# A two-layer diffusion backbone on one core: the first adaLN group in blocks of 128 channels, the S5 setup behind the modulation, and two adaLN groups moved from layer 0 to layer 1

## The chip, the cores and the metric

The kernel runs as one program on one core of a Trainium2 chip. The metric is device time in microseconds of one execution; the times below are of three executions. One execution was also taken with the hardware profiler, and all rows are from that one.

## The reference, cut to what matters

Two layers work on 256 context tokens and 256 latent tokens of 1024 channels, in float32. Every layer begins with the adaLN parameters, six rows of 1024 numbers for each of the two streams:

```
mod = silu(cond) @ w_ada + b_ada          # (1024) @ (1024 x 6144), for c and for c_ctx
h   = layer_norm(x) * (1 + mod[1]) + mod[0]
z   = h @ w_in                            # S5, latent attention, window attention, three gates
y   = merge(s5(z0), mla(z1..3), window(z4..6), gates(z7)) @ w_out
x   = layer_norm(ALPHA * x + mod[2] * y)
f   = expert_choice_ffn(layer_norm(x) * (1 + mod[4]) + mod[3])     # 16 experts, SwiGLU
x   = layer_norm(ALPHA * x + mod[5] * f)
```

Only `mod[0]` (shift) and `mod[1]` (scale) are needed for `h`; the other four are needed after the mixers. Layer 1 updates the latent stream alone. The S5 mixer also needs tables made of its own parameters (discretised states, products of B and C with powers), which depend on no token: the code calls their making the S5 setup.

## The kernel before, in words

`build` runs the layers one after the other. `w_ada` of one layer is 24 MB; it is used in three groups of 8 MB, group 0 for `mod[0:2]`, group 1 for `mod[2:4]`, group 2 for `mod[4:6]`. `ada_group` takes a group in eight steps of 1 MB. Step k holds input channels 128k to 128k+127 for all 2048 outputs of the group, so no output is complete before the eighth step; then the bias is added, four transposes follow, and `modT` is written. A step is 16 matmuls with 32 columns of `silu(cond)` as the weights.

Group 0 of layer 0 is made at the very start, into seven tiles of its own and two buffers of `stg`, a ring of four buffers of 512 KB that all weights of `w_in` pass through too. The four `x` tiles are loaded after the fifth step's weights. `layer` then loads the rest of the constants (`const[:, 128:]`, 985 KB), and `modulated_split` does the layer norm, and for each channel block k transposes, scales and shifts it and splits it into a high and a low part (`h`); after every second block the closure `step` of `s5_product` issues two blocks of the S5 input product, 24 matmuls (12 for each block).

`s5_setup` is a generator in two parts. The first part (small operations on 32 columns) is traced at the very start. The second part, which builds B and C products in the blocks `big0` to `big2`, is traced after the S5 product and its transposes (`s5_inputs`), and ahead of `proj_tok`, which projects the attention inputs. `s5_main`, the S5 scan in eight turns, needs everything of it.

The build step makes a list schedule for each engine: of the instructions that are ready in its own time model, the one traced earliest goes first. So work traced later moves forward into idle time unless something holds it, and loads whose buffers are free leave in the order of the code. `keep_in_program_order` pins an instruction behind the one traced before it on its engine. SyncE issues all loads. PSUM tiles come from named sets; "sc" has two, "tp" two, "ad" one.

The other adaLN groups are queued in `adaq`. The gate and branch matmuls are queued in `fillq`, and `tick` in the S5 and attention loops issues some of them. In `step` each piece of fill work adds its modelled time to `ada_debt`, and adaLN steps (1.6 each) are issued until the debt is paid. Five groups stand in the queue of layer 0 (its own 1 and 2, and all three of layer 1), none in layer 1. `drain(True)` issues what is left at the end of the mixers. 16 KB per partition at the top of the arena, called "late", are reserved for what comes after the mixers, and hold nothing until then.

After the mixers come the output projection, the router and the 16 experts (12 MB of weights each, loaded through buffers that become free one by one).

Of the kernel before, what the change touches and what calls it, by code (L numbers as in the profile page):

```python
# [15 lines left out]
KT = 8  # L16
DEPTH = 2
# [140 lines left out]
class Net:  # L158
# [48 lines left out]
    def step(self):  # L207
        try:
            us = next(self.fillq[0])
            self.debt -= us  # L210
            self.ada_debt += us
        except StopIteration:
            self.fillq.pop(0)
        while self.adaq and self.ada_debt > 0:
            try:
                self.ada_debt -= next(self.adaq[0])
            except StopIteration:
                self.adaq.pop(0)
# [129 lines left out]
        nc.vector.tensor_scalar(self.sc.rearrange("p (k s) -> p k s", s=32)[:, :, 0:2],  # L348
                                t2.rearrange("p (k s) -> p k s", s=2), 0.5, None, op0=OP.mult)

    def ada_group(self, l, g, bufs=None):

        nc = self.nc
        R = self.adarow[(l + g) % 2]
        self.load(R, self.ins["b_rep"][l, g])
        pt = self.ps("ad")
        scv = self.sc.rearrange("p (k s) -> p k s", s=32)
        src = self.ins["w_ada"][l, g]
        for k in range(KT):
            if bufs and k < 7:  # L360
                self.load(bufs[k], src[k])
                ws = [bufs[k][:, 0:1024], bufs[k][:, 1024:2048]]
            else:
                ws = []
                for h in range(2):
                    ws.append(self.stg())
                    self.load(ws[h], src[k, :, 1024 * h:1024 * h + 1024])
            for h in range(2):
                for j in range(4):

                    i = self.mm(pt[32 * j:32 * j + 32, 256 * h:256 * h + 256], scv[:, k, :],
                                ws[h][:, 256 * j:256 * j + 256], k == 0 and h == 0, k == KT - 1)
                    if k == 0 and h + j:
                        self.tc.keep_in_program_order(i)
            yield 1.6
        nc.vector.tensor_tensor(R, pt, R, op=OP.add)
        tp = self.ps("tp")
        for b in range(4):
            self.tr(tp[:, b * 128:(b + 1) * 128], R[:, b * 128:(b + 1) * 128])
        tv = tp.rearrange("p (b jj jm s) -> p jj jm b s", b=4, jj=2, jm=2)  # L380
        for jj in range(2):
            m = 2 * g + jj
            dst = self.modT[l % 2][:, m].rearrange("p (jm b) s -> p jm b s", jm=2)
            self.nc.vector.tensor_copy(dst, tv[:, jj, :, :, 0:2])
            if m in (1, 4):
                nc.vector.tensor_scalar(self.modT[l % 2][:, m], self.modT[l % 2][:, m], 1.0, None, op0=OP.add)
        self.adaR[l % 2, g] = True
        yield 0.0

    def mod_row(self, l, m, s, dst, scale=1.0):  # L390
# [77 lines left out]
    def modulated_split(self, l, x, in_place, step, stats):  # L468

        nc = self.nc  # L470
        mt = self.modT[l % 2]
        xns = {}
        for t in range(4):
            xns[t] = x[t] if in_place[t] else self.buf(f"xn{t}", D)
            if t in stats:
                self.ln_final(xns[t], x[t], *stats[t])
            else:
                self.ln_apply(xns[t], x[t])
        step(None, None)
        hh, hl = [self.block(f"h{r}", F32R).rearrange("p (k n) -> p k n", k=KT) for r in range(2)]  # L480
        part = lambda k, c: (hh[:, k, c], hl[:, k, c])
# [2 lines left out]
        units = [(k, s) for k in range(KT) for s in range(2)] if l == 0 else [(k, s) for s in range(2) for k in range(KT)]  # L484
        for u in range(0, 16, 2):
            (k, s), (k1, s1) = units[u:u + 2]
            if s1 and k1 > 2 and k1 % 2:
                step(part, (k1 - 3) // 2)
            tp, h = self.ps("tp"), tmps()
            for i, (k, s) in enumerate(units[u:u + 2]):  # L490
                for t in range(2):
                    self.tr(tp[:, 256 * i + 128 * t:256 * i + 128 * t + 128], xns[2 * s + t][:, k * 128:(k + 1) * 128])
            for i, (k, s) in enumerate(units[u:u + 2]):
                c = slice(256 * i, 256 * i + 256)
                scale, shift = mt[:, 1, k, s:s + 1], mt[:, 0, k, s:s + 1]
# [9 lines left out]
        step(part, 3)  # L505
        self.unrot(htmp=3)
        self.free(*[f"xn{t}" for t in range(4) if not in_place[t]])
        return part
# [2 lines left out]
    def s5_setup(self, l, S, NP):  # L511

        nc = self.nc
        v, g = nc.vector, nc.gpsimd
        bg = [self.block(f"big{i}", F32) for i in range(3)]
        CE = S["CE"] = [t[:, 0:2560].rearrange("p (d j e h) -> p d j e h", d=2, j=16, e=5) for t in bg[:2]]
        BM = S["BM"] = [[t.rearrange("p (j c) -> p j c", j=16) for t in ts]
                        for ts in ([t[:, 2560:3584] for t in bg[:2]], [bg[2][:, 1024 * d:1024 * d + 1024] for d in range(2)])]
        MM = S["MM"] = [t[:, 3584:4096].rearrange("p (x q c) -> p x q c", x=2, q=4) for t in bg[:2]]
# [22 lines left out]
        n = [0]  # L542
# [63 lines left out]
        v.scalar_tensor_tensor(fr, kk, MAGIC, fr, op0=OP.subtract, op1=OP.subtract)  # L606
        v.tensor_scalar(S["fr"], fr, -1.0, None, op0=OP.mult)
        yield
        load_part(0)
        QQ = part(64).rearrange("p (r d j) -> p r d j", r=2, d=2)  # L610
        qrv, qiv = QQ[:, 0], QQ[:, 1]
        v.tensor_copy(QQ[:, 0].rearrange("p d j -> p (d j)"), qr)
        v.tensor_copy(QQ[:, 1].rearrange("p d j -> p (d j)"), qi)
        KX = part(4 * 112).rearrange("p (q i h) -> p q i h", q=4, i=7)
        BB = part(64 * NP).rearrange("p (r d j h) -> p r d j h", r=2, d=2, j=NP)
        X1 = part(64 * NP).rearrange("p (k j h) -> p k j h", k=4, j=NP)
# [1073 lines left out]
    def build(self, layers=(0, 1), stop=None):  # L1690
# [3 lines left out]
        with tc.tile_pool(name="main", bufs=1) as main, \  # L1694
# [12 lines left out]
            self.adaR, self.OH, self.ah, self.cd, self.back, self.norm, self.rw, self.rrow = {}, {}, {}, {}, {}, {}, {}, {}  # L1707
            self.buf("late", 4096, at=self.LATE)
            self.adarow = [self.buf(f"ada{i}", 512, low=True) for i in range(2)]
            x = {t: self.buf(f"x{t}", D, low=True) for t in range(4)}  # L1710
            self.ada_start()
# [5 lines left out]
            hb = [self.block(f"h{i}", F32) for i in range(2)]  # L1717
            bufs = [hb[i // 2][:, 2048 * (i % 2):2048 * (i % 2) + 2048] for i in range(4)]
            bufs += [self.block(f"extra{i}", F32)[:, 0:2048] for i in range(2)] + [self.buf("wada", 2048, True)]
            for k, _ in enumerate(self.ada_group(layers[0], 0, bufs)):  # L1720
                if k == 4:
                    for t in range(4):
                        self.load(x[t], self.xin(t))
                if k in (7, 8):
                    kc = len(self.early)
                    self.early.append(self.wload(self.w_in(layers[0], 0, 512)[:, 2 * kc:2 * kc + 2], 2, 512))
            self.free("wada")
            for l in layers:
                self.layer(l, x, 1 if l == 0 and 1 in layers else None)
            for t in (2, 3):  # L1730
                self.load(self.out[0, (t - 2) * 128:(t - 1) * 128], x[t])

    def xin(self, t):
        return self.ins["ctx" if t < 2 else "x"][0, (t % 2) * 128:(t % 2) * 128 + 128]

    def layer(self, l, x, nxt):
        tc, nc = self.tc, self.nc
        full = l == 0
        q0 = 0 if full else 256
        N = 512 - q0  # L1740
        with tc.tile_pool(name=f"parts{l}", bufs=1, reuse_waits="tile") as self.R:
            if l:
                self.stg = self.rot("stg", 1024, 3, at=20288)
            step, pts = self.s5_product(l)
            if (l % 2, 1) not in self.adaR:
# [5 lines left out]
                pass  # L1751
            S = self.S
            Z = self.proj_tok(l, h, full)
            if (l % 2, 1) not in self.adaR:
                self.adaq += [self.ada_group(l, 1), self.ada_group(l, 2)]
            if nxt is not None:
                self.adaq += [self.ada_group(nxt, g) for g in range(3)]
            mT = self.buf("mT", KT * N, True, 12416 if full else None).rearrange("p (k n) -> p k n", k=KT)
            self.fill(self.gates(l, h, 0, mT, q0))
            if not full:  # L1760
# [78 lines left out]
        with tc.tile_pool(name=f"late{l}", bufs=1, reuse_waits="tile") as pool:  # L1839
# [22 lines left out]
            self.T = {}  # L1862
            tts = (0, 1, 2, 3) if full else (2, 3)
            self.free(*[n for n in self.A.live if n[0] in "EF"])
            self.buf("late", 4096, at=self.LATE)
            self.finish(l, x, pts, nxt is not None)

    ARENA_COLS = 27456
# [19 lines left out]
def _prepare(inputs):  # L1888
# [11 lines left out]
    a["w_ada"] = f("w_ada").reshape(DEPTH, KT, 128, 3, 4, 2, 256).transpose(0, 3, 1, 2, 5, 4, 6).reshape(DEPTH, 3, KT, 128, 2048)  # L1900
# [54 lines left out]
```

## Time and profile before

| | |
|---|---|
| median of three executions | 2099.42 us (2098.45 to 2099.58) |
| the profiled execution's own time | 2097.34 us |
| its span, first to last instruction | 2095.6 us |
| busy in the span: TensorE matmul | 1791.9 us (86%) |
| VectorE | 1042.9 us (50%) |
| ScalarE | 611.3 us (29%) |
| GpSimd | 451.5 us (22%) |
| read from HBM | 541 MB |

PE is TensorE's matmuls, PEld its weight loads, DVE is VectorE, ACT ScalarE, POOL GpSimd, and SPq the queue of SyncE, which issues the loads. An engine's busy share is a mean over stages that have different limits, so the stretches of the rows further down are to be read one by one. In them, the granted clock is TensorE's as a share of full speed, and the DMA share is the mean over the 16 DMA engines. Most matmuls are on the helper's line 243 and most loads on line 229, so a group is told apart by the tiles that it names.

### The profile page before, as it was taken

To read this page: it belongs to the slowest core of one execution; us is meant where nothing else is said; L and a number is where in the kernel's file an instruction comes from. 1 tells how busy PE (TensorE), PEld (TensorE's weight loads), DVE (VectorE), ACT (ScalarE), POOL (GpSimd) and SP (SyncE) were. 2 spreads that over 40 slices of the span, in tenths; PEclk is the share of its full clock that TensorE was granted. 3 is DMA by queue.
4 is the path that set the end of the run, shared out by engine and by line. 5 is a ranking of instruction groups with operands and counts; after the bars stand their busy time and mean duration, and the time that the engine had idled before them with its cause. 6 is when DMAs were issued, how large, how long until landed. Compare 5 with 4: busy or idle time off the path is not lost.

```text
span 2095.6 us, 31733 instructions
## 1 busy us (share of the span) xinstructions
PE 1791.9 (86%) x12425; PEld 1112.2 (53%) x12425; DVE 1042.9 (50%) x2431; ACT 611.3 (29%) x1353; POOL 451.5 (22%) x590
## 2 busy tenths in 40 slices
PE   5899899999999699999799979799998776676765
PEld 2876666677777544434233368787786532232221
DVE  6767666756528712313555367977767321010102
ACT  2444253344424311101111165654553110000000
POOL 5735320011125100001343034641114000000000
PEclk8999999999999799999999989999999888776777
DMA  9236744522247689999999733342267799999996
GB/s 334 67 123 218 245 144 163 163 78 71 60 132 274 248 354 421 421 421 416 416 413 351 297 91 94 81 129 63 76 214 297 291 420 421 421 421 421 420 421 272
DMA packets 173013, 544.20 MB, mean 260 GB/s; under 512 B 18624, under 2 KB 101696, under 8 KB 122816
## 3 DMA queue, kind: packets, MB, share of 16 engines
q1 hardware_dynamic: 172864, 542.18, 68.2%
q8 instruction: 98, 1.61, 0.3%
q14 instruction: 51, 0.42, 0.1%
HBM read 541.09 MB, written 1.05 MB: 259 GB/s over the span
## 4 chain that ended last, share of the span: by engine, by line
PE 54%; DMA 23%; DVE 14%; POOL 3%; ACT 3%; issue 3%; SPq 0%; POOLq 0%; ACTq 0%; DVEq 0%
PE sc L243 16%; PE mm L243 16%; PE F L243 13%; DMA arena<-in_w_down 4%; DMA arena<-in_w_up 4%; PE tp L246 4%; PE ad L243 4%; DMA arena<-in_w_gate 3%; DVE extra L852 2%; DVE wc L407 2%; DMA h<-in_w_gate 2%; DMA big<-in_w_gate 2%; DMA arena<-in_w_in 1%; DMA extra<-in_w_up 1%; DMA extra<-in_w_gate 1%
## 5 line engine op out<-in xcount | busy, mean ns | idle before, releaser
L243 PE MATMUL F<-h,wc 128*128 128x256 f32 (+1 forms) x1200 | 237.1, 350 | 11.3 <-ACT arena L1295 9.0
L404 ACT ACTIVATE wc<-arena 128x512 fp32r<-128x512 f32 (+2 forms) x280 | 169.9, 619 | 208.6 <-DMA arena<-in_w_in 45.8
L407 DVE TENSOR_TENSOR wc<-arena,wc 128x512 fp32r<-128x512 f32 (+2 forms) x205 | 163.3, 808 | 112.9 <-ACT wc L404 112.5
L243 PE MATMUL sc<-arena,xs 128*32 128x256 f32 (+1 forms) x1336 | 188.5, 522 | 33.7 <-DMA arena<-in_w_up 20.5
L243 PEld LDWEIGHTS F<-h,wc 128*128 128x128 f32 x1200 | 188.5, 196 | 42.6 <-ACT arena L1295 9.9
L243 PE MATMUL mm<-arena 128*32 128x256 f32 (+5 forms) x1244 | 186.1, 467 | 21.9 <-DMA arena<-in_w_down 13.4
L246 PE MATMUL tp<-const,arena 128*128 128x128 f32 (+2 forms) x819 | 137.5, 293 | 70.4 <-DVE arena L1618 11.6
L1641 DVE TENSOR_TENSOR arena<-mm,arena 32x512 f32<-32x512 f32 (+1 forms) x128 | 70.9, 554 | 219.0 <-PE mm L243 217.4
L407 POOL TENSOR_TENSOR wc<-arena,wc 128x512 fp32r<-128x512 f32 (+2 forms) x75 | 96.9, 1292 | 376.3 <-ACT wc L404 316.7
L246 PEld LDWEIGHTS tp<-const,arena 128*128 128x128 f32 (+2 forms) x819 | 97.3, 147 | 130.5 <-issue 38.5
L238 ACT ACTIVATE arena<-tp 128x512 f32<-128x512 f32 (+3 forms) x142 | 61.9, 463 | 341.7 <-PE tp L246 297.4
L260 POOL TENSOR_TENSOR lnq<-lnq,k 128x1 f32<-128x1 f32 x22 | 16.5, 750 | 568.8 <-DVE lnq L307 530.0
L243 PEld LDWEIGHTS sc<-arena,xs 128*32 128x32 f32 (+1 forms) x1336 | 60.8, 131 | 139.7 <-issue 68.7
L243 PEld LDWEIGHTS mm<-arena 128*32 128x32 f32 (+2 forms) x1244 | 76.3, 137 | 107.2 <-issue 50.5
L243 PE MATMUL sc<-h,xs 128*32 128x256 f32 (+1 forms) x752 | 112.3, 533 | 21.0 <-DMA h<-in_w_gate 13.2
L1618 DVE TENSOR_TENSOR arena<-arena,sc 128x512 f32<-128x512 f32 (+1 forms) x32 | 17.7, 554 | 178.2 <-PE sc L243 177.9
L243 PE MATMUL sc<-big,xs 128*32 128x256 f32 (+1 forms) x632 | 80.8, 487 | 25.2 <-DMA big<-in_w_gate 13.0
L1616 ACT ACTIVATE arena<-sc 128x512 f32<-128x512 f32 (+1 forms) x32 | 15.7, 491 | 295.1 <-PE sc L243 295.1
L243 PE MATMUL mm<-wc,h 128*128 128x512 f32 (+2 forms) x288 | 79.1, 399 | 11.3 <-ACT h L496 4.4
L243 PE MATMUL F<-extra,wc 128*128 128x256 f32 (+1 forms) x432 | 85.7, 343 | 3.5 <-DVE arena L1330 3.1
L1617 DVE SCALAR_TENSOR_TENSOR arena<-arena,sc 128x512 f32<-128x512 f32 (+1 forms) x32 | 17.7, 554 | 142.3 <-ACT arena L1616 142.2
L243 PEld LDWEIGHTS sc<-h,xs 128*32 128x32 f32 (+1 forms) x752 | 36.8, 133 | 89.2 <-issue 60.7
(344 smaller groups left out, 3183.1 us busy)
## 6 DMA issues: line engine op xcount, KB each, us to landing
arena<-in_w_up SPq DMA_DIRECT2D x65, 1024.0 KB, 16.8
arena<-in_w_down SPq DMA_DIRECT2D x61, 1024.0 KB, 19.8
arena<-in_w_gate SPq DMA_DIRECT2D x48, 1024.0 KB, 19.7
arena<-in_w_ada SPq DMA_DIRECT2D x82, 512.0 KB, 5.0
h<-in_w_gate SPq DMA_DIRECT2D x41, 1024.0 KB, 15.0
arena<-in_w_in SPq DMA_DIRECT2D x66, 512.0 KB, 4.0
big<-in_w_up SPq DMA_DIRECT2D x26, 1024.0 KB, 19.8
h<-in_w_down SPq DMA_DIRECT2D x26, 1024.0 KB, 18.6
```

Source lines behind the costliest of these rows:

```text
L238: self.nc.scalar.activation(out, in_, AF.Copy)
L243: return self.nc.tensor.matmul(out, lhsT, rhs, start=start, stop=stop, skip_group_check=True)
L246: self.nc.tensor.transpose(out, in_, self.c("idn")[:n, :n])
L260: self.nc.gpsimd.tensor_tensor(out, in_, e.to_broadcast(list(in_.shape)), op=OP.pow)
L404: nc.scalar.activation(hi, src, AF.Copy)
L407: eng.tensor_tensor(lo, src, hi.bitcast(F32), op=OP.subtract)
L852: v.tensor_tensor_scan(z, rb, z, 0.0, op0=OP.mult, op1=OP.add)
L1616: nc.scalar.activation(th, gu[0][:, :NF], AF.Tanh, scale=0.5)
L1617: v.scalar_tensor_tensor(th, th, 1.0, gu[0][:, :NF], op0=OP.add, op1=OP.mult)
L1618: v.tensor_tensor(th, th, gu[1][:, :NF], op=OP.mult)
L1641: v.tensor_tensor(YS[n][o:o + 32, c * NF:(c + 1) * NF], yp[r:r + 32, :NF], m5[r:r + 32], op=OP.mult)
```

## The change

1. **First group in blocks.** The weights of group 0 of layer 0 are laid out anew: tile b holds all 1024 input channels for outputs 128b to 128b+127 of shift and scale. `ada_first` is a generator; each call makes one block: eight matmuls, a copy to SBUF, two small matmuls that add the four row groups and turn the result, and one addition of the bias from a small new array `b_t` into `modT`. `modulated_split` calls it ahead of each channel block. The `x` tiles are loaded first, then the eight tiles of weights into `big0` to `big2`, `extra0`, `extra1` and "late", with the first two chunks of `w_in` among them. Two of the four layer norms of layer 0 are applied by ScalarE in place of VectorE.
2. **S5 setup behind the modulation.** The blocks `big0` to `big2` are taken for the setup only at the start of its second part, and in layer 0 the two copies at its head are pinned behind what VectorE was given before them.
3. **Groups of layer 1.** Layer 0 queues three groups (its own 1 and 2, and group 0 of layer 1), layer 1 queues its groups 1 and 2. Their loads go through buffers of their own in "late" (four in layer 0, three in layer 1) in place of `stg`. The debt grows by 0.35 of the fill time in layer 0 and by 0.2 in layer 1.

```diff
             us = next(self.fillq[0])
             self.debt -= us
-            self.ada_debt += us
+            self.ada_debt += us * self.ADA
...
-    def ada_group(self, l, g, bufs=None):
+    def ada_first(self, l, tiles):
+
+        nc = self.nc
+        v = nc.vector
+        own = self.buf("adafirst", 532)
+        bt, two = own[:, 512:528].rearrange("p (m k) -> p m k", m=2), own[:, 528:530]
+        self.load(bt, self.ins["b_t"])
+        v.tensor_scalar(bt[:, 1], bt[:, 1], 1.0, None, op0=OP.add)
+        v.tensor_reduce(two, self.c("idn").rearrange("p (j s) -> p s j", j=4)[:, 0:2], axis=AX.X, op=OP.add)
+        scv = self.sc.rearrange("p (k s) -> p k s", s=32)
+        for b in range(KT):
+            pt = self.ps("sc")
+            for r in range(2):
+                for j in range(4):
+                    k = 4 * r + j
+                    self.mm(pt[32 * j:32 * j + 32, 0:256], scv[:, k, :], tiles[b][:, 256 * k:256 * k + 256], r == 0, r == 1)
+            R = own[:, 256 * (b % 2):256 * (b % 2) + 256]
+            self.copy(R, pt[:, 0:256], "v")
+            for m in range(2):
+                self.mm(pt[:, 256 + 2 * m:258 + 2 * m], R[:, 128 * m:128 * m + 128], two, True, True)
+            v.tensor_tensor(self.modT[l % 2][:, 0:2, b], pt[:, 256:260].rearrange("p (m s) -> p m s", m=2),
+                            bt[:, :, b, None].to_broadcast([128, 2, 2]), op=OP.add)
+            yield
+        self.free("adafirst")
+
+    def ada_group(self, l, g):
...
-            if bufs and k < 7:
-                self.load(bufs[k], src[k])
-                ws = [bufs[k][:, 0:1024], bufs[k][:, 1024:2048]]
-            else:
-                ws = []
-                for h in range(2):
-                    ws.append(self.stg())
-                    self.load(ws[h], src[k, :, 1024 * h:1024 * h + 1024])
+            ws = []
+            for h in range(2):
+                ws.append(self.astg())
+                self.load(ws[h], src[k, :, 1024 * h:1024 * h + 1024])
...
-                self.ln_apply(xns[t], x[t])
+                self.ln_apply(xns[t], x[t], "va"[t % 2])
...
             (k, s), (k1, s1) = units[u:u + 2]
+            next(self.first, None)
...
-        v.tensor_copy(QQ[:, 0].rearrange("p d j -> p (d j)"), qr)
-        v.tensor_copy(QQ[:, 1].rearrange("p d j -> p (d j)"), qi)
+        for i, q in enumerate((qr, qi)):
+            c = v.tensor_copy(QQ[:, i].rearrange("p d j -> p (d j)"), q)
+            if NP == 16:
+                self.tc.keep_in_program_order(c)
...
-            self.buf("late", 4096, at=self.LATE)
+            late = self.take_late(4)
...
-            for k, _ in enumerate(self.ada_group(layers[0], 0, bufs)):
-                if k == 4:
-                    for t in range(4):
-                        self.load(x[t], self.xin(t))
-                if k in (7, 8):
+            for t in range(4):
+                self.load(x[t], self.xin(t))
+            tiles = []
+            for i in range(3):
+                big = self.block(f"big{i}", F32)
+                tiles += [big[:, c:c + 2048] for c in range(0, int(big.shape[1]), 2048)]
+            tiles += [self.block(f"extra{i}", F32)[:, 0:2048] for i in range(2)] + [late[:, 0:2048]]
+            for k in range(KT):
+                self.load(tiles[k], self.ins["w_ada"][layers[0], 0, k])
+                if k in (1, 3):
                     kc = len(self.early)
                     self.early.append(self.wload(self.w_in(layers[0], 0, 512)[:, 2 * kc:2 * kc + 2], 2, 512))
-            self.free("wada")
+            self.first = self.ada_first(layers[0], tiles)
...
+        self.ADA = 0.35 if full else 0.2
...
-            if (l % 2, 1) not in self.adaR:
-                self.adaq += [self.ada_group(l, 1), self.ada_group(l, 2)]
+            self.adaq += [self.ada_group(l, 1), self.ada_group(l, 2)]
             if nxt is not None:
-                self.adaq += [self.ada_group(nxt, g) for g in range(3)]
+                self.adaq.append(self.ada_group(nxt, 0))
...
-            self.buf("late", 4096, at=self.LATE)
+            self.take_late(3)
```

## Rows read from the trace of the kernel before

**Rows 1.** Stretches: busy PE, PEld, DVE, ACT, POOL; clock, DMA share, GB/s

```profile
38.90:78.70 39.80, 31.50 (x120) 27.30 (x120) 39.74 (x64) 14.09 (x30) 35.41 (x36) 0.91 0.38 112
78.70:134.00 55.30, 55.30 (x453) 51.71 (x452) 27.34 (x55) 26.36 (x62) 19.98 (x24) 1.00 0.27 82
134.00:256.00 122.00, 108.08 (x1117) 72.75 (x1116) 91.96 (x155) 43.46 (x81) 63.21 (x74) 0.97 0.65 216
256.00:420.00 164.00, 160.49 (x968) 106.31 (x968) 107.61 (x296) 71.18 (x188) 22.11 (x23) 0.99 0.52 165
1270.00:1380.00 110.00, 90.61 (x976) 82.95 (x976) 96.93 (x165) 62.12 (x117) 68.32 (x82) 0.92 0.39 107
1380.00:1560.00 180.00, 171.11 (x1178) 145.62 (x1177) 132.53 (x346) 99.97 (x242) 34.33 (x33) 0.97 0.34 101
1560.00:1660.00 100.00, 77.55 (x546) 58.04 (x548) 64.83 (x144) 33.97 (x71) 29.07 (x26) 0.90 0.72 275
1660.00:2060.00 400.00, 274.87 (x2973) 112.33 (x2968) 53.43 (x128) 19.88 (x46) 0.00 (x0) 0.76 1.01 421
```

**Rows 2.** SyncE's queue in order of time: start, us, what it issued

```profile
5.59 1.12 SPq L229 DMA_DIRECT2D arena<-in_ctx  x2
...
23.08 0.34 SPq L229 DMA_DIRECT2D const<-in_const  x1
...
33.75 0.33 SPq L229 DMA_DIRECT2D bglu<-in_s_bg  x1
```

**Rows 3.** DMA issues of the first 60 us: count, KB, median us to landing

```profile
arena<-in_ctx SPq DMA_DIRECT2D x2, 512.0 KB, 14.6
...
const<-in_const SPq DMA_DIRECT2D x1, 985.0 KB, 14.5
...
arena<-in_b_rep SPq DMA_DIRECT2D x3, 256.0 KB, 8.2
...
bglu<-in_s_bg SPq DMA_DIRECT2D x1, 2.0 KB, 7.3
```

**Rows 4.** Chain of waits, first 260 us: start, us, what

```profile
37.18 0.57 ACT h L496
...
84.11 0.87 PE tp L246 x8
...
134.35 1.04 PE sc L243 x16
...
231.32 4.88 DMA arena<-in_w_ada
...
236.95 5.67 DMA arena<-in_w_in
...
251.64 5.45 DMA arena<-in_w_in
```

**Rows 5.** The same chain later: 24 matmuls of a gate

```profile
604.79 5.60 PE F L243 x24
```

**Rows 6.** S5 setup's VectorE operations, 36 to 96 us: min/median/max ns

```profile
L550 DVE TENSOR_TENSOR arena<-arena x46: 407/723/1504, 39.9 to 87.1; 128x256 f32<-128x256 f32 x46
L550 DVE TENSOR_TENSOR big<-arena x8: 410/628/949, 48.0 to 87.5; 128x256 f32<-128x256 f32 x8
```

**Rows 7.** S5 setup's GpSimd operations in the same stretch

```profile
L551 POOL TENSOR_TENSOR arena<-arena x34: 622/802/1067, 41.4 to 93.0; 128x256 f32<-128x256 f32 x34
L551 POOL TENSOR_TENSOR big<-arena x8: 797/896/1180, 43.3 to 89.8; 128x256 f32<-128x256 f32 x8
```

**Rows 8.** GpSimd in order of time: the setup's last products

```profile
90.94 2.85 POOL L551 TENSOR_TENSOR arena<-arena 128x256 f32<-128x256 f32 x4
```

**Rows 9.** The adaLN matmuls alone, by stretch

```profile
134.00:256.00 122.00, 26.99 (x368) 9.77 (x368) 0.00 (x0) 0.97 0.65 216
256.00:420.00 164.00, 22.29 (x272) 7.62 (x272) 0.00 (x0) 0.99 0.52 165
```

More of the change, by code (lines that the diff above doesn't have):

```diff
@@ L386, in ada_group @@
                 nc.vector.tensor_scalar(self.modT[l % 2][:, m], self.modT[l % 2][:, m], 1.0, None, op0=OP.add)
-        self.adaR[l % 2, g] = True
         yield 0.0
@@ L505, in modulated_split @@
         step(part, 3)
+        next(self.first, None)
         self.unrot(htmp=3)
@@ L514, in s5_setup @@
         v, g = nc.vector, nc.gpsimd
[L515 to L519, printed above, removed]
         S["rho"] = rho = self.small.tile([128, 32], F32, name="s5rho", bufs=1)
@@ L608, in s5_setup @@
         yield
+        bg = [self.block(f"big{i}", F32) for i in range(3)]
+        CE = S["CE"] = [t[:, 0:2560].rearrange("p (d j e h) -> p d j e h", d=2, j=16, e=5) for t in bg[:2]]
+        BM = S["BM"] = [[t.rearrange("p (j c) -> p j c", j=16) for t in ts]
+                        for ts in ([t[:, 2560:3584] for t in bg[:2]], [bg[2][:, 1024 * d:1024 * d + 1024] for d in range(2)])]
+        MM = S["MM"] = [t[:, 3584:4096].rearrange("p (x q c) -> p x q c", x=2, q=4) for t in bg[:2]]
         load_part(0)
@@ L1706, in build @@
             self.A = Arena(arena, self.ARENA_COLS)
-            self.adaR, self.OH, self.ah, self.cd, self.back, self.norm, self.rw, self.rrow = {}, {}, {}, {}, {}, {}, {}, {}
-            self.buf("late", 4096, at=self.LATE)
+            self.OH, self.ah, self.cd, self.back, self.norm, self.rw, self.rrow = {}, {}, {}, {}, {}, {}, {}
+            late = self.take_late(4)
             self.adarow = [self.buf(f"ada{i}", 512, low=True) for i in range(2)]
@@ L1716, in build @@
             self.stg = self.rot("stg", 1024, 4, True)
-            hb = [self.block(f"h{i}", F32) for i in range(2)]
-            bufs = [hb[i // 2][:, 2048 * (i % 2):2048 * (i % 2) + 2048] for i in range(4)]
-            bufs += [self.block(f"extra{i}", F32)[:, 0:2048] for i in range(2)] + [self.buf("wada", 2048, True)]
-            for k, _ in enumerate(self.ada_group(layers[0], 0, bufs)):
-                if k == 4:
-                    for t in range(4):
-                        self.load(x[t], self.xin(t))
-                if k in (7, 8):
+            for t in range(4):
[8 more added lines that the diff above has]
+                if k in (1, 3):
                     kc = len(self.early)
                     self.early.append(self.wload(self.w_in(layers[0], 0, 512)[:, 2 * kc:2 * kc + 2], 2, 512))
-            self.free("wada")
+            self.first = self.ada_first(layers[0], tiles)
             for l in layers:
@@ L1731, in build, with take_late, nxt @@
                 self.load(self.out[0, (t - 2) * 128:(t - 1) * 128], x[t])
+    def take_late(self, n):
+        late = self.buf("late", 4096, at=self.LATE)
+        bufs = [late[:, i:i + 1024] for i in range(4096 - 1024 * n, 4096, 1024)]
+        if n < 4:
+            self.adarow = [late[:, 0:512], late[:, 512:1024]]
+        at = [0]
+        def nxt():
+            at[0] += 1
+            return bufs[(at[0] - 1) % n]
+        self.astg = nxt
+        return late
     def xin(self, t):
@@ L1744, in layer @@
             step, pts = self.s5_product(l)
-            if (l % 2, 1) not in self.adaR:
+            if full:
                 self.load(self.const[:, 128:], self.ins["const"][:, 128:])
@@ L1753, in layer @@
             Z = self.proj_tok(l, h, full)
-            if (l % 2, 1) not in self.adaR:
-                self.adaq += [self.ada_group(l, 1), self.ada_group(l, 2)]
+            self.adaq += [self.ada_group(l, 1), self.ada_group(l, 2)]
             if nxt is not None:
-                self.adaq += [self.ada_group(nxt, g) for g in range(3)]
+                self.adaq.append(self.ada_group(nxt, 0))
             mT = self.buf("mT", KT * N, True, 12416 if full else None).rearrange("p (k n) -> p k n", k=KT)
@@ L1898, in _prepare @@
     a["c2"] = np.stack([cc.reshape(KT, 128), c.reshape(KT, 128)], -1).transpose(1, 0, 2).reshape(128, KT * 2)
-    a["w_ada"] = f("w_ada").reshape(DEPTH, KT, 128, 3, 4, 2, 256).transpose(0, 3, 1, 2, 5, 4, 6).reshape(DEPTH, 3, KT, 128, 2048)
+    a["w_ada"] = f("w_ada").reshape(DEPTH, KT, 128, 3, 4, 2, 256).transpose(0, 3, 1, 2, 5, 4, 6).reshape(DEPTH, 3, KT, 128, 2048).copy()
+    a["w_ada"][0, 0] = f("w_ada")[0].reshape(KT, 128, 6, KT, 128)[:, :, 0:2].transpose(3, 1, 0, 2, 4).reshape(KT, 128, 2048)
+    a["b_t"] = f("b_ada")[0].reshape(6, KT, 128)[0:2].transpose(2, 0, 1)
     b = f("b_ada").reshape(DEPTH, 3, 4, 1, 512)
```

## The prediction

> **What bounds the kernel now.** I read the stretches first, then the chain of waits inside those that the change touches, then the queue that feeds them. Three kinds of stretch are to be seen [rows 1]. From 1660 us to the end the loads set the pace: the DMA engines are busy throughout at 421 GB/s, so whatever delays the last release of a weight buffer moves the end by as much, and so does whatever advances it. From 256 to 420 us TensorE is busy for 160.5 of 164 us: work taken away there is time won. Between them lie stretches where VectorE is nearly or wholly full: the S5 product (38.9 to 78.7 us, VectorE 39.7 of 39.8, TensorE 31.5), the S5 scan of layer 0 (134 to 256, VectorE 92.0 and TensorE 108.1 of 122) and that of layer 1 (1270 to 1380, VectorE 96.9 of 110, TensorE 90.6).
>
> The chain of waits gives the marks of the start. The first scaled block is written at 37.18 us; one set of eight transposes takes 0.87 us; the first S5 matmul of the scan comes at 134.35; and between 231 and 257 us three loads stand on the chain, 4.88 us for adaLN weights and 5.67 and 5.45 us for `w_in` [rows 4]. The last two wait in the same four buffers that the adaLN steps fill twice a step.
>
> **The start: are the blocks used as they come?** The new code lets channel block 0 be modulated when its tile has landed. But the bias `b_t` is loaded inside `ada_first`, whose body starts in `modulated_split`, so its load is traced after the eight tiles, both early chunks and the 985 KB of constants. In the queue of before, loads with free buffers left in the order of the code, and a load that left late came late: the context tiles issued at 5.59 us took 14.6 us, the constants issued at 23.08 us took 14.5, and the 2 KB of the S5 gate's bias, issued at 33.75, took 7.3 [rows 2, 3]. So a small load does not pass the large ones ahead of it. The constants landed at 23.08 + 14.5 = 37.6 us; the new order has the same bytes ahead of them less the 256 KB bias of the old group [rows 3], which at 421 GB/s [rows 1] is 0.6 us. I put `b_t` at 37.0 us, and the first scaled block at 37.5, against 37.18 before: no gain. With two "sc" tiles, blocks 0 and 1 wait there for their bias and blocks 2 to 7 wait behind them.
>
> [...]
>
> What is won at the start is contention. The S5 product needs 96 matmuls and 64 transposes; at 5.60 us for 24 [rows 5] and 0.87 for eight [rows 4] that is 22.4 + 7.0. The block form adds some 64 matmuls of 256 columns for the old 128; at 26.99 / 368 = 0.073 us [rows 9], 4.7 us, of which three quarters (3.5) lie behind the bias. Before, the product took 41.5 us from the first scaled block to 78.7, where 29.4 would do, because VectorE also did most of 54 setup operations (median 0.6 to 0.7 us) and GpSimd most of 42 (0.8 to 0.9) [rows 6, 7]. After, only those that make the C tables (24 and 24) can move ahead of the pinned copies, once the first tiles are freed. Lower bound of the end: 37.5 + 2 (lead) + 22.4 + 3.5 + 5.3 (the six blocks of transposes left) = 70.7; upper bound, if sharing goes on as before, 78.7 + 3.5 = 82.2. I take 74.5, nearer to the lower, since half of the shared work has gone.
>
> **The pinned setup.** Behind the last scaling, which I put 7 us ahead of the product's end as the last work on the path (67 us), stand 30 VectorE operations and 18 of GpSimd, and behind these the transposes of the B tables and the scan's first matmul. 30 x 0.7 = 21 us of VectorE [rows 6], with some 4 us of weight splits between: done at 92. Before, GpSimd's last of them ended at 90.94 + 2.85 = 93.8 [rows 8]. So the setup comes out level. The scan then starts by the later of two: product end + (134.35 - 78.7 = 55.7, TensorE without a gap [rows 1]) = 130.2, or 92 + (134.35 - 93.8 = 40.6) = 132.6. Term A: **-2** (bounds -8, if the product ends at 70.7 and the setup no later than that asks, and +8, if the product ends at 82). ScalarE's work for two layer norms ends before the bias is there and is put at nothing.
>
> **Layer 0 with two groups less.** A group is 128 matmuls: five take 26.99 + 22.29 = 49.3 us in the two stretches [rows 9], 9.9 each, with four transposes (0.44) 10.3. Two less: 20.6 us of TensorE. By the debt the scan (eight gates, 8 x 5.1 x 0.35 = 14.3 us of debt) now carries one group where it carried about three, and the two left stand from 256 us on as two did before. So all of the saving is in the stretch 134 to 256. There TensorE falls to 108.1 - 20.6 = 87.5 us, under VectorE's 92.0; VectorE's floor allows -30. On the chain the adaLN work and the three late loads (16.0 us [rows 4]) are what goes, but the scan's own path through VectorE, GpSimd and ScalarE stays. Bounds: -8 (only the adaLN load and a few of its matmuls were on the path) and -30. Term B: **-18**, by the 16.0 us of loads and a few matmuls beside them. All later stretches of layer 0, its experts too, are released by this and shift as one.
>
> **Layer 1 with two groups more.** 20.6 us of TensorE and 16 MB of loads come in between 1270 and 1660 us. The loads have room (107 and 101 GB/s of 421 [rows 1]); they are issued on the same queue as `w_in`, each in front of a later one by 512 KB / 421 GB/s = 1.2 us at most. TensorE sits idle 19.4 us in the scan, 8.9 from 1380 to 1560, 22.5 from 1560 to 1660 [rows 1]. The fill work of layer 1 is half as long: 92.4 us in the model, x 0.2 = 18.5, 11 to 12 of 16 steps; the last four are issued by the drain. Five to six are issued in the scan, where VectorE is the fuller engine; what moves forward into its gaps costs nothing, what is left stands in the 1380 to 1560 stretch, which has few gaps. Bounds: 0 (all 20.6 in idle time) and +21 (none). I take **+8**: six steps in the scan and part of the drain hidden, the rest (some 13 us) partly so.
>
> **Sum.** -2 - 18 + 8 = -12 on the profiled run's own time of 2097.34 us (span 2095.6) gives 2085.3. The median of the runs shown is 2.1 above that, which would make it 2087.4. I forecast **2086**. No change that a measurement here can tell is what lies within 0.2%, 4.2 us, of the time before.
>
> **Rivals.** *The bias overtakes and the blocks are used as they come.* The last tile has 1241 KB less ahead of it than the constants had, and lands at 37.6 - 3.0 = 34.6 us; two blocks of product (5.6) and the lead put the bound at 44; TensorE's own work of 22.4 + 7.0 + 4.7 = 34 us, from 15 us on (the first tile, by its 3.2 MB against the constants' 12.6), puts it at 50. The product would end 28 us early, the scan start at 50 + 55.7 = 106. 2097 - 28 - 18 + 8 = **2059**. For it: nothing in the chain but the bias prevents it. Against: the 7.3 us of the 2 KB load [rows 3].
>
> *The moved work costs in layer 1 what it gives in layer 0.* If the steps of layer 1 stay where they are issued, TensorE pays all 21 us: 2097 - 2 - 18 + 21 = **2098**. For it: 171.1 of 180 us busy from 1380 on [rows 1]. Against: 19.4 us idle ahead of that.
>
> *The pinned setup becomes the bound; the kernel gets slower.* It is late from the scan's first matmul. If the C tables can't move forward either, because their blocks are freed only as the last adaLN blocks are done, all 54 and 42 operations stand behind 67 us: 54 x 0.7 = 38 us and the splits put them at 110, the scan at 110 + 40.6 = 151, 16 us late; and the waiting GpSimd and VectorE then also share with the projections. With A = +16 to +24, 2097 + 20 - 18 + 8 = **2107**. It decides the sign once the scan starts after 134.35 + 10 = 144 us. For it: VectorE has no idle time in the product's stretch [rows 1], so pinned work must be added at its end. Against: only two copies are pinned.
>
> **Chances.** The forecast, 2070 to 2094: 0.50. Blocks as they come: 0.12. The even exchange, 2093 to 2101: 0.21, of which 0.06 faster, 0.10 same, 0.05 slower. The late setup: 0.17, of which 0.03 within 0.2%. So faster 0.68, same 0.13, slower 0.19. The forecast's own range is 2070 to 2094; leaving out the low end of the first rival and the upper half of the last (together under 0.2) gives 2062 to 2105.
>
> **What would show it.** The load of `b_t` late in SyncE's queue and landing near 37 us, with TensorE idle ahead of that; the first scaled block near 37.5; the S5 product's end near 74; the scan's first matmul near 132; its length down from 122 to about 104 us; no `w_in` load on the chain after it; layer 0's experts ending some 20 us earlier; and layer 1 from its start to the saturated loads some 8 us longer. I am wrong if `b_t` lands before 20 us, if the setup's last GpSimd product ends after 105, or if layer 1 grows by 20.

## The result, and the profile after

The changed kernel takes **2119.46 us** (median; 2118.51 to 2121.41) against 2099.5 for the kernel before, measured beside it (2098.45 to 2101.68): a ratio of 1.0095, interval 1.0077 to 1.0112. It is slower by 20 us; the forecast was 2086, and 2119 lies outside its range.

Where the 22.8 us between the two spans (2095.6 and 2118.4) arise is read from the first or last start of a few operations in the two traces, in us:

| mark | before | after | difference |
|---|---|---|---|
| first scaled block | 37.18 | 36.46 | -0.7 |
| last scaled block | 68.6 | 78.4 | +9.8 |
| first scan operation of layer 0 | 137.9 | 143.1 | +5.2 |
| last scan operation of layer 0 | 241.9 | 241.7 | -0.2 |
| first scaled block of layer 1 | 1213.0 | 1203.7 | -9.3 |
| first scan operation of layer 1 | 1274.9 | 1265.2 | -9.7 |
| last scan operation of layer 1 | 1371.9 | 1406.8 | +34.9 |
| last softmax operation of layer 1 | 1570.6 | 1593.4 | +22.8 |
| last tanh of the experts of layer 1 | 2058.3 | 2080.0 | +21.7 |

Layer 0 gains 9.3 us and layer 1 loses 31, all of it in its S5 scan, which grows from 97.0 to 141.6 us; 12 us come back behind it, since work that stood there has already been done. The row of the scan's operations in layer 1 (count; shortest, median and longest in ns; first and last start), and the adaLN matmuls alone in the stretches of layer 1 [rows 1 has the stretches]:

```profile
L876 DVE TENSOR_TENSOR_SCAN extra<-s5rho,extra x64: 390/414/1434, 1265.2 to 1406.8; 128x128 f32<-128x128 f32 x64
```

```profile
1270.00:1380.00 110.00, 20.24 (x256) 5.54 (x256) 0.00 (x0) 0.95 0.79 244
1380.00:1560.00 180.00, 0.00 (x0) 0.00 (x0) 0.00 (x0) 0.91 0.26 77
```

All 256 matmuls of the two moved groups run inside the scan, and none after it. They cost 20.2 us of TensorE, about what was forecast (20.6); the scan lost 44.6. What the engines do in four pieces of it (busy TensorE, weight load, VectorE, ScalarE, GpSimd; clock, DMA share, GB/s):

```profile
1300.00:1320.00 20.00, 20.00 (x238) 14.86 (x238) 16.32 (x30) 8.96 (x14) 10.51 (x14) 1.00 0.94 313
1320.00:1340.00 20.00, 15.61 (x127) 11.94 (x126) 6.31 (x15) 7.83 (x12) 2.71 (x2) 0.83 0.64 209
1340.00:1360.00 20.00, 20.00 (x180) 16.04 (x178) 4.27 (x7) 7.79 (x16) 5.13 (x4) 1.00 1.04 333
1360.00:1380.00 20.00, 20.00 (x223) 16.47 (x223) 12.14 (x24) 7.00 (x23) 8.25 (x12) 1.00 0.60 161
```

VectorE, 96.9 of 110 us busy in this scan before [rows 1], does 4.27 of 20 us here. TensorE is full in three of the four pieces, but not with the scan: it runs gates (`F<-h,wc`) and adaLN steps in turn. The timeline of TensorE up to where that ends (start, us, what), one row of VectorE's, and ScalarE's copies out of PSUM for the scan's tails, by form:

```profile
1321.73 0.66 PE L246 MATMUL tp<-const,arena 128*128 128x128 f32 x4 [0.94 <-DVE arena L397]
...
1361.83 3.14 PE L243 MATMUL F<-h,wc 128*128 128x256 f32 x24
1364.81 0.82 PE L246 MATMUL tp<-const,arena 128*128 128x128 f32 x6
1365.44 3.02 PE L243 MATMUL F<-h,wc 128*128 128x256 f32 x23
1368.31 0.27 PE L246 MATMUL tp<-const,arena 128*64 128x128 f32 x1
```

```profile
1324.97 0.25 DVE L405 COPY modT<-tp 128x16 f32<-128x16 f32 x2
```

```profile
L238 ACT ACTIVATE arena<-tp x19: 254/262/390, 1365.9 to 1417.9; 64x128 f32<-64x128 f32 x16, 128x256 f32<-128x256 f32 x3
L238 ACT ACTIVATE arena<-mm x16: 206/218/227, 1291.1 to 1413.4; 128x64 f32<-128x64 f32 x16
```

The first tail of the scan leaves its accumulators ("mm") at 1291.1 us, but its two transposes ("tp") come out at 1365.9. The six transposes at 1364.81 are the four that close the second adaLN group and then these two. Each of the scan's eight turns has a head (input products and the scan operations) and a tail (output products, two transposes, copies), which the code issues one turn later; on the chip the first tail waited 75 us, until the last of the 32 adaLN loads had been used. The first group's tile, written at 1321.73 us, was read out by VectorE at 1324.97, so for the last 40 us the tail did not wait for a full tile. The reading that fits is that the tiles of a set are given out in the order of the code, and the second group's, which stood ahead, was not used before 1364.81.

The start, in the chain of waits (start, us, what; pieces left out at "..."):

```profile
19.17 16.81 DMA arena<-in_b_t
36.46 0.57 ACT h L517
...
78.36 0.57 ACT h L517
...
139.53 1.04 PE sc L243 x16
```

The bias is late as forecast and lands at 36.0. The last block is scaled at 78.4 and not at 67, and the scan's first matmul comes at 139.53 and not at 132 [rows 4 has 134.35 for before].

### The profile page after: what moved, and what is told of

It is laid out like the page before. It is cut to its first block, busy times and chain, and to the rows that moved or that the text cites. A ratio compares the mean times of both kernels' runs of the same rounds, so it can differ in the third digit from the quotient of the medians.

```text
span 2118.4 us, 31774 instructions
## 1 busy us (share of the span) xinstructions
PE 1807.8 (85%) x12453; PEld 1122.1 (53%) x12453; DVE 1037.6 (49%) x2445; ACT 609.9 (29%) x1351; POOL 443.5 (21%) x590
## 4 chain that ended last, share of the span: by engine, by line
PE 55%; DMA 22%; DVE 15%; ACT 3%; issue 2%; POOL 2%; SPq 0%; POOLq 0%; ACTq 0%; DVEq 0%
PE sc L243 17%; PE mm L243 16%; PE F L243 14%; DMA arena<-in_w_down 5%; PE ad L243 4%; PE tp L246 4%; DMA arena<-in_w_up 3%; DMA arena<-in_w_gate 3%; DVE wc L427 2%; DVE extra L876 2%; DVE arena L567 2%; DMA big<-in_w_gate 2%; DMA h<-in_w_gate 2%; DMA extra<-in_w_gate 1%; DMA big<-in_w_up 1%
## 5 line engine op out<-in xcount | busy, mean ns | idle before, releaser
L243 PE MATMUL sc<-arena,xs 128*32 128x256 f32 (+1 forms) x1336 | 188.1, 522 | 34.5 <-DMA arena<-in_w_up 21.7
L243 PEld LDWEIGHTS mm<-arena 128*32 128x32 f32 (+2 forms) x1244 | 76.6, 136 | 110.3 <-issue 49.2
## 6 DMA issues: line engine op xcount, KB each, us to landing
h<-in_w_gate SPq DMA_DIRECT2D x41, 1024.0 KB, 14.5
```

The costliest lines, as they stand in the source:

```text
L243: return self.nc.tensor.matmul(out, lhsT, rhs, start=start, stop=stop, skip_group_check=True)
```

## The experiments

The theory formed on these rows has two links. *The debt:* once layer 0's three groups are issued, `step` goes on adding to `ada_debt` though nothing is in the queue. Counted in the program, 26.28 us of debt stand when layer 1 begins; the 16 steps of its two groups ask 16 x 1.6 = 25.6. So the first gate of layer 1 issues both groups at once, ahead of the second head and the first tail. *The PSUM tile:* each group closes with a "tp" tile, and there are two; the first tail's tile is the third in line. The rival was plain contention: 8 MB of loads and 128 matmuls to a group cost what they cost, wherever they stand. The runs are numbered in the order in which they were made, as the expectations count them, and told in the order of the argument.

**Run 1: the debt set to zero.**

```
         self.ADA = 0.35 if full else 0.2
+        self.ada_debt = 0.0
```

> One line: the adaLN debt is set to zero as each layer begins. Theory A (left-over debt): after layer 0's groups are issued the debt goes on growing with every fill step and stands at 26.28 us when layer 1 begins, more than the 16 steps x 1.6 = 25.6 of its two groups, so the first gate issues both at once; with the debt at zero they are spread over the layer. The scan of layer 1, first to last scan operation, falls from 141.6 us to 97 to 110, the adaLN matmuls between 1280 and 1400 from 244 to under 110, and the time from 2119 to 2090 to 2101. Theory B (contention: loads and matmuls of two groups cost the same wherever they stand): the scan gets shorter but the later stretches longer by as much, 2112 to 2120.

Measured: 2107.35 us, ratio to before 1.0029 (1.0017 to 1.0041). The scan falls to 103.9 us, and the loads no longer stop it; but the time lies between the two theories. The steps are spread as the code says: 77 of the 256 matmuls run up to the scan's last operation (1366.4 us) and 179 behind it, 120 of them in the first row here (the adaLN matmuls alone); there TensorE has no time to give, the second (all work):

```profile
1400.00:1480.00 80.00, 10.39 (x120) 3.24 (x120) 0.00 (x0) 0.98 0.44 146
```

```profile
1425.00:1470.00 45.00, 45.00 (x346) 33.62 (x346) 32.60 (x105) 18.78 (x53) 3.83 (x3) 0.99 0.42 140
```

From layer 1's first scaled block to its last softmax it takes 379.2 us, against 357.6 before and 389.7 in the changed kernel. The debt was the cause of the order, then, but the order that was meant is nearly as dear: 20 us for the layer, all that the two groups ask of TensorE.

**Run 2: the debt left, the closing transposes in another PSUM tile.**

```
-        tp = self.ps("tp")
+        tp = self.ps("ad" if l and g else "tp")
```

> The debt stays and both groups are issued at once, but the four closing transposes of layer 1's two groups write the PSUM bank of their own accumulator ('ad') and no longer a 'tp' tile. Theory A, the PSUM part of it: what stops the scan is that the first tail's 'tp' tile stands behind the two groups' closing 'tp' tiles and so behind all 32 loads; freed of that, tails run between the loads, the scan of layer 1 takes 100 to 115 us and the time is 2090 to 2103. Theory B (TensorE's order or the load queue is simply full of adaLN work): the scan stays at 130 to 142 us and the time at 2112 to 2120.

Measured: 2098.02 us, ratio 0.9991 (0.9979 to 1.0002). Both groups are still issued at once and all 256 matmuls still run within the scan; only the tile is another. The scan's row, one of the four pieces, the adaLN matmuls alone, and ScalarE's timeline:

```profile
L876 DVE TENSOR_TENSOR_SCAN extra<-s5rho,extra x64: 391/418/1443, 1264.9 to 1375.2; 128x128 f32<-128x128 f32 x64
```

```profile
1340.00:1360.00 20.00, 17.35 (x235) 12.55 (x232) 16.63 (x28) 11.00 (x19) 10.74 (x14) 1.00 0.80 258
```

```profile
1255.00:1400.00 145.00, 20.06 (x256) 5.49 (x256) 0.00 (x0) 0.96 0.67 208
```

```profile
1290.92 0.33 ACT L238 ACTIVATE arena<-mm 128x64 f32<-128x64 f32 x2
1295.08 0.41 ACT L238 ACTIVATE arena<-tp 64x128 f32<-64x128 f32 x2
```

The first tail's transposes come 4 us behind its accumulators in place of 75. VectorE is back at 16.63 of 20 us, and the scan takes 110.3. So 31 of the 44.6 us are the wait for a PSUM tile; the other 13 are the groups' own work. Contention as the cause of the stall is refuted: the loads move in the same stretch at the same pace (190, 272 and 215 GB/s from 1262 to 1300, on to 1340 and on to 1380 us, against 187, 261 and 247 in the changed kernel; the last lands at 1358.2 us, against 1360.5).

**Run 3: part 3 alone undone.** All five groups in layer 0 at the old rate, none in layer 1.

```
-        self.ADA = 0.35 if full else 0.2
+        self.ADA = 1.0
...
-            self.adaq += [self.ada_group(l, 1), self.ada_group(l, 2)]
-            if nxt is not None:
-                self.adaq.append(self.ada_group(nxt, 0))
+            if full:
+                self.adaq += [self.ada_group(l, 1), self.ada_group(l, 2)]
+                self.adaq += [self.ada_group(nxt, g) for g in range(3)]
```

> Part 3 alone undone: all five groups in layer 0 at the old rate of 1.0, none in layer 1; the first group in blocks, the setup's place and the adaLN loads' own buffers stay. If the loss lies in layer 1 alone, layer 1 (modulation to last tanh) takes the 845 us of before and not the 876 of after. Layer 0: if taking two groups away was worth what the marks say (14.5 us from the scan's first matmul on), the modulation of layer 1 comes at 1213 + 5 = 1218 and the time is 2101 to 2105; if the separate buffers and not the missing groups gave that, it comes near 1204 and the time is 2087 to 2092.

Measured: 2109.08 us, ratio 1.0044 (1.0030 to 1.0059). Layer 1 takes 845.7 us, as before. Layer 1's modulation comes at 1224.6, later than either case that I gave: parts 1 and 2, with the separate buffers of part 3, make layer 0 11.6 us longer, 3.8 of it ahead of the scan's first operation (141.7) and 7.8 behind it.

**Run 9: the same with shared buffers.** As run 3, with `self.stg()` in place of `self.astg()` in `ada_group`, to see whether the separate buffers are those 7.8 us.

> As the third run (five groups in layer 0, none in layer 1), but the adaLN loads go back to the four buffers that they shared with the w_in loads. What is left of the change is then the first group in blocks and the setup's place. In the third run layer 0 was 7.8 us longer from the first scan operation to layer 1's modulation than before (1082.9 against 1075.1). If the separate buffers did that, those 1082.9 go back to 1075 to 1077 and the time is 2100 to 2104. If they are innocent (it is the order in which blocks and setup leave layer 0), they stay at 1081 to 1085 and the time at 2106 to 2112.

Measured: 2108.41 us, ratio 1.0040 (1.0023 to 1.0058); from the first scan operation to layer 1's modulation 1080.9 us. The buffers are innocent. Against the changed kernel's 1060.6 this prices two groups less in layer 0 at 20.3 us; against run 3's 1082.9, where the buffers are the changed kernel's too, it is 22.3. The 5.8 us by which 1080.9 is above 1075.1 of before are not settled: loads stand on the chain from 205 to 272 us for 5.54, 7.68 and 6.03 us where before it was 4.88, 5.67 and 5.45 [rows 4], which is 3.3 of them.

**Run 7: the issue rate.** Debt zero, and layer 1's steps issued at 1.0 of the gates' time, so that they stand in the code within the scan.

```
-        self.ADA = 0.35 if full else 0.2
+        self.ADA = 0.35 if full else 1.0
+        self.ada_debt = 0.0
```

> As the first run (debt zero as each layer begins), but layer 1's groups are issued at 1.0 and not 0.2 of the gates' time, so that both stand in the code within the scan's gates. If what a group costs depends on the stretch it stands in (full price, some 20 us, where TensorE has no gaps after the scan; half of that in the scan, where VectorE is the fuller engine), the scan takes 106 to 114 us, the stretches after it are as before, and the time is 2095 to 2100, like the second run. If spreading is innocent and the two groups cost 20 us anywhere, it stays at 2104 to 2110.

Measured: 2097.93 us, ratio 0.9996 (0.9981 to 1.0012). The scan takes 114.9 us, a little above the 106 to 114 expected, and from the first scaled block to the last softmax it is 368.7, against 379.2 at 0.2. The closing "tp" tiles now stand between later tails and stop none for long. So it is the place that sets the price: over the whole layer some 10 us when all steps stand in the scan, 20 when spread. TensorE's idle time within the scan shows what is used: 16.9 us before, 16.4 in run 1, 11.1 in run 2 and 9.8 here.

**Run 4: the bias first.** Debt zero, and `b_t` loaded ahead of the tokens and the tiles into the same arena columns (claimed earlier).

```
+            self.own = self.buf("adafirst", 532)
+            self.load(self.own[:, 512:528].rearrange("p (m k) -> p m k", m=2), self.ins["b_t"])
             for t in range(4):
                 self.load(x[t], self.xin(t))
```

> The line of the first run, and the 8 KB bias loaded ahead of the tokens and tiles. Theory A' (the late bias held the blocks): block 0 is modulated when its tile lands, some 17 us earlier than at 36.5; TensorE then has 34 us of work from about 20 us on, the product ends at 50 to 60 against 82.6, the scan starts at 110 to 118 against 139.5, and the time is 20 to 28 us under that of the first run. Rival (VectorE's setup is the bound: 54 operations of 0.7 us and the pinned copies stand behind the last scaling and in front of the scan): the scan starts at 128 to 135, the time is only 5 to 12 us under the first run.

Measured: 2105.58 us, ratio 1.0024 (1.0011 to 1.0036), 1.8 under run 1. The bias lands 1.8 us after its issue, blocks are scaled from 21.8 us on (36.4 in run 1), the last at 60.6 (77.0); but the scan's first operation is only 5.9 us earlier, at 135.8, just later than the rival's 128 to 135, and the time falls by less than its 5 to 12 us. Part of this is a new wait, in the timelines of GpSimd, TensorE and VectorE:

```profile
62.70 10.77 POOL L524 TENSOR_TENSOR h<-arena,h 128x512 fp32r<-128x512 f32 x1 [1.32 <-DVE arena L517]
```

```profile
73.52 1.24 PE L243 MATMUL mm<-wc,h 128*128 128x512 f32 x2 [9.62 <-POOL h L524]
```

```profile
63.55 2.76 DVE L566 TENSOR_TENSOR arena<-arena 128x256 f32<-128x256 f32 x8
66.23 0.41 DVE L566 TENSOR_TENSOR big<-arena 128x256 f32<-128x256 f32 x1
66.57 2.76 DVE L566 TENSOR_TENSOR arena<-arena 128x256 f32<-128x256 f32 x8
```

The last subtraction for `h`, on GpSimd, takes 10.77 us while VectorE runs setup operations without a gap, and TensorE waits 9.62 us for it. (The profiled execution took 2096.81 us at a granted clock of 0.924; the other nine, 2101.65 to 2109.09, had 0.914 to 0.919, so its marks are not those of the median.)

**Run 5: the bias first and the other PSUM tile.** The edits of run 4 (without the zeroed debt) and of run 2.

> The two edits that helped, together: the bias ahead of the tiles (as in the fourth run) and the closing transposes in the accumulator's bank (as in the second). If the two costs are independent, the marks add: the scan of layer 0 starts near 136 and that of layer 1 takes 110 us, the time is 2098 - 6 = 2092 (2088 to 2095). If the earlier start is lost again on the way (TensorE's granted clock falls with the earlier start, or a load is waited for instead), it is 2096 to 2099.

Measured: 2090.97 us, ratio 0.9957 (0.9939 to 0.9974), 7.0 under run 2. By the marks of run 4 (5.9 us) the two costs add; by the medians of runs 4 and 1 the early bias was worth only 1.8, and most of run 4's executions had the lower clock (0.914 to 0.919; in run 1 it was 0.917 to 0.926). The scan of layer 0 begins at 134.7, that of layer 1 takes 111.5 us.

**Run 6: the last subtraction on VectorE.** As run 5, and

```
-            (nc.gpsimd if u % 4 else nc.vector).tensor_tensor(lo, h, hi.bitcast(F32), op=OP.subtract)
+            (nc.gpsimd if u % 4 and (l or u < 14) else nc.vector).tensor_tensor(lo, h, hi.bitcast(F32), op=OP.subtract)
```

> As the run before, and the last of layer 0's eight subtractions that make the low halves of h moves from GpSimd to VectorE. Theory C (blocked GpSimd): with the bias first, that subtraction stood 10.78 us on GpSimd, against 1.29 in the run of the change, while VectorE ran 27 setup operations without a gap, and TensorE waited 9.6 us for it; on VectorE it takes 0.7 us, the product ends near 66 in place of 75.4, the scan starts 7 to 9 us earlier, at 124 to 128, and the time is 2080 to 2086. Rival D (the setup behind it is the bound anyway): the setup's last GpSimd product still ends at 104 and the 33 to 40 us from there to the scan stay: it starts at 134 to 140 and the time is within 3 us of the run before.

Measured: **2083.21 us** (four executions, 2077.15 to 2088.46), ratio 0.9918 (0.9892 to 0.9944): faster than both kernels. Both theories hold in part. TensorE's wait is gone and the product ends at 66.4, 8.3 earlier; but the scan starts only 2.3 us earlier, at 132.4. TensorE's timeline at the product's end, and the chain of waits behind it:

```profile
65.03 0.87 PE L243 MATMUL mm<-wc,h 128*128 128x512 f32 x2 [1.13 <-DVE h L524]
```

```profile
65.68 4.77 DVE arena L566 x6
...
71.22 3.21 DVE arena L566 x8
74.76 2.01 DVE arena L566 x6
...
92.78 1.97 PE tp L246 x8
```

From 65 to 92 us the chain is now VectorE's setup with the weight splits between, so the setup has become the bound (rival D): TensorE waits 1.03, 0.49 and 2.60 us there, where it has no such wait in run 5. The profiled spans differ by 4.6 us, 2.3 of them here; the rest arises between the scan and the experts of layer 0, and I have no cause for it.

**Run 8: no pin.** As run 2, without `keep_in_program_order` on the two copies.

> As the second run, without the pin on the two copies that hold the setup's B tables behind the modulation. If the pinned setup sets the scan's start (the third rival of the prediction), its operations move forward into the wait for the bias, and the scan starts 3 to 10 us earlier than 139.5. If the product sets it, VectorE is shared again during the product, and the scan starts at 139 or later.

Measured: 2110.77 us in one execution. The scan's first operation comes at 153.2, 10.2 later than in run 2 (143.0), and the last scaled block at 86.0 in place of 78.4. Without the pin all of the setup shares VectorE with the product again (the setup's GpSimd products start from 42.1 to 92.6 us, and in run 2 up to 105.5). So the pin was not the bound of the changed kernel's start; it earned 10 us.

## Why the prediction was wrong, point by point

**The step that failed is layer 1 with two groups more**, term C: forecast +8 (bounds 0 to +21), measured +31.0 (876.3 against 845.3 us from the first scaled block to the last tanh); a growth by 20 was named as a sign of being wrong. "Five to six are issued in the scan" took the debt to begin at zero. It began at 26.28 us, all 16 steps were issued at the first gate, and their closing "tp" tiles held the scan's tails until the last load had landed. The rows of before could not show this, since layer 1 had no group to pay such a debt with; the code of `step`, which I had read, could. The prediction has no rival for it: none of its bounds holds an order of instructions that stops a tail.

**The term would have failed without the debt too.** With the debt at zero the layer takes 865.4 us, +20.1, the price of the rival "the moved work costs in layer 1 what it gives in layer 0". I had counted part of the steps behind the scan as hidden; TensorE is full there (45.00 of 45 us). The +8 that I took is what is seen when all steps stand in the scan: layer 1 of run 2 takes 854.9 us, +9.6.

**Layer 0 with two groups less**, term B: forecast -18, measured -20.3 with the start and the setup alike on both sides (run 9; -22.3 against run 3). The reading of the debt in layer 0 and the price of 10.3 us a group held, and none of the 25 longest pieces of the changed kernel's chain between 200 and 262 us is a load, as forecast. From before it is only -14.5, because parts 1 and 2 cost 5.8 us more behind the scan's start, which the prediction had at nothing. Where the saving arises did not hold: "all of the saving is in the stretch 134 to 256". The scan carries 16.1 us less of adaLN matmuls than before (6.71 for 22.79), but from its first to its last scan operation it takes 98.7 us against 104.0 before and 106.3 in run 9, only 7.6 of the 20.3; the other 12.7 come behind it. That the size came out near is in part luck.

**The start**, term A: forecast -2 (bounds -8 to +8), measured +5.2. The late bias was right: landing at 36.0 for 37, first scaled block 36.46 for 37.5. The step that failed is the product's end, "I take 74.5, nearer to the lower": it was 82.8, beyond the upper bound of 82.2. Two terms were too small. The block form's matmuls were counted in the code, 64 in all, and priced by the trace, where each stands as two (128, as for the old group): 96 of them run behind the first scaled block, 9.66 us of TensorE for the 3.5 of the sum. At the sum's own price the right count alone is 3.5 us more and makes the bounds 74.2 and 85.7. The other is the sharing. The split of the setup was counted rightly, 24 operations of each engine during the product and 30 and 18 behind it; but half the sharing then cost three quarters of the whole (8.6 of 11.5 us). In the pieces that the chain of waits prints from 36 to 83 us VectorE has 28.3 us and TensorE 10.5: the scalings and splits wait in VectorE's queue among the table products. TensorE is busy for 41.41 of the 46.34 us as well, so that VectorE alone set the pace is read from the chain; no run shows it.

The pinned setup's last GpSimd product starts at 105.6 and ends at 106.6 (an end after 105 was named beforehand as a sign of being wrong), for 92; yet product end + 55.7 = 138.5 is still nearly what the scan kept (139.5). The chain does run through the setup from 79 to 95.5 us, but TensorE works beside it, from the product's end to the scan, with one wait of 0.95 us, for a weight split that stands behind setup operations on VectorE:

```profile
82.80:139.53 56.73, 55.78 (x455) 51.67 (x456) 35.29 (x68) 29.59 (x68) 25.45 (x30) 1.00 0.33 87
```

```profile
95.53 2.24 PE L243 MATMUL mm<-wc,h 128*128 128x416 f32 x10 [0.95 <-DVE wc L427]
```

So the product set the start and not the pin, which cost about 1 us there; the rival of the late setup is refuted by this and by run 8.

**The bias that overtakes**, the first rival, did not come: 16.81 us from issue to landing behind the tiles in the changed kernel, 1.8 when first (run 4). The 985 KB of constants issued just ahead of it landed at 16.68 + 19.1 = 35.8 us, the bias at 36.0: it did not pass them, and the rows of before had it right. The price of that rival was wrong as well: with the blocks used as they come, 7.0 us are won and not 28 (run 5 against run 2), because the last subtraction, 10.77 us on GpSimd, and then VectorE's setup are next in line; with the subtraction moved too (run 6) it is 14.8.

**Sum.** +5.2 + 5.8 - 20.3 + 31.0 = +21.7, and 1.1 more behind the last tanh make the 22.8 us between the spans. Without the stall, C is about +9.6 and the whole is even, which run 2 shows: 2098 against 2099.

## What to carry to other kernels

When a change lets a producer run in a place where it never ran, look for state that the old program left behind unused: here a debt counter. Whatever is traced early claims its place in every ring that it shares, PSUM tiles too, and a short tile claimed at the end of a long chain of loads holds all that is traced after it (here for 31 of the 44.6 us that the scan lost); give such work a tile of its own, or issue it later. Filler work was cheap here only where another engine was the fuller one (some 10 us for two groups within the scan, 20 when spread), so its place in the code was worth more than its even spreading; and what is taken out of a stretch is won only if the next in line there leaves room (in run 6 VectorE's setup left 2.3 us of the product's 8.3).

## What the hardware showed that I had not expected

A GpSimd subtraction of 128x512 took 10.77 us in run 4, against 1.29 for the same operation in the changed kernel, while VectorE ran 27 setup operations and one weight split back to back; in run 5 it took 10.77 us again. The setup operations took 0.41 us each, one starting every 0.34 us, where the same operations have a median of 0.84 us while both engines work (36 to 79 us of the changed kernel). The last three setup operations of that stretch, from 71.60 us on, took 2.15 us together, where three at that pace take 1.09, and ended 0.28 us after the subtraction. That the two engines held each other up is my reading of the two timelines; by what means, no run shows. What it cost is shown: TensorE waited 9.62 us for the subtraction in run 4 and 9.64 in run 5; in run 6, which moved the one operation to VectorE, it took 1.10 us there and TensorE waited 1.13.
